# Splitting FFN weights by two GpSimd DMAs and one ScalarE pass

## The chip, the core and the metric

The kernel runs on one core of a Trainium2 chip. The metric is the time of one execution on the device, in microseconds, taken as the median of several runs. A core has engines that run side by side and meet through semaphores: TensorE (PE in the profile, PEld for its weight loads), VectorE (DVE), ScalarE (ACT), GpSimd (POOL) and SyncE (SP), and 16 DMA engines that move data between HBM and SBUF. Each engine works through its own instructions in a fixed order; an instruction whose inputs are late holds up all that stand behind it on that engine.

## The reference: what is computed

Two trunk layers over 512 tokens of width 1024, in float32. The first mixes tokens by attention (four global and four windowed heads, 256 context tokens beside them), the second by a Fourier transform over tokens and channels. Each layer ends with a gated ConvFFN of width 2816, and every sub-layer lies between RMS norms with shift, scale and gate from a conditioning vector. The change lies in the ConvFFN:

```
def conv_ffn(h, w_up, conv_w, conv_b, w_down):
    u = h @ w_up                                  # 512 x 1024 times 1024 x 5632
    up = jnp.pad(u, ((0, 0), (1, 1), (0, 0)))
    u = up[:, :-2] * conv_w[0] + up[:, 1:-1] * conv_w[1] + up[:, 2:] * conv_w[2] + conv_b
    gate, val = jnp.split(u, 2, axis=-1)
    return (jax.nn.silu(gate) * val) @ w_down     # 512 x 2816 times 2816 x 1024
```

## The kernel before

**Products in two parts.** TensorE multiplies numbers of the rounded type float32r. To keep float32 accuracy each operand is split into a high part h (the value rounded to float32r) and a low part l (what the rounding left, rounded again), and a product is the sum of three matmuls, h h, h l and l h, into one PSUM bank. `mm3` (lines 97 to 99) issues them: L97 and L98 read the high part of the weights, L99 the low part. For the weights the high part is called `wh`, the low part `wl`.

**The split.** `split` (line 119) makes both parts from a float32 tile: ScalarE copies the tile into h with the rounding cast, and VectorE (or, where a call says so, GpSimd) subtracts h from the tile into l. Both are recorded on line 120. `held` ties an instruction behind the last fence that was set on its engine, so that the planner doesn't draw it ahead of a norm between two sub-layers.

**Weights and their buffers.** A weight tile goes from HBM into a buffer `raw` (line 127, three buffers of up to 8 KB per partition, loads issued by SP), is split into a pair `wh`, `wl` (line 132, five pairs of 4 KB each), and is multiplied. The three `raw` buffers are shared by everything that is loaded to be split: up weights, down weights, the weights of the attention and the Fourier layer, the sums that a seven-product step makes of its weights, and the tiles of the modulation matrix that VectorE multiplies in a GEMV (lines 388 and 391). Buffers of one name are given out in program order, each as soon as one comes free.

**The FFN.** `ffn` (line 1057 on) runs over 22 chunks fi of 128 inner channels. For each chunk there is a gate and a value tile of `w_up`, 1024 x 128 each (512 KB), loaded as one tile of 1 MB. A chunk is computed in one of two ways. A *plain* step takes the two tiles with 24 matmuls of 512 columns each. A *seven-product* step (`seven_products`) takes both tiles together as a 2 x 2 block product with seven block products instead of eight: VectorE makes sums of weight blocks in a second `raw` buffer, four pairs are split from them, and there are 84 matmuls of 256 columns, with copies of PSUM halves by ScalarE (lines 1020 to 1030) between them. The list `SEVEN` names the chunks of the second kind: 5, 6, 8, 10, 12, 14, 15, 17, 18, 20 in layer 0, and 8, 9, 11, 12, 14, 15, 17, 18, 20 in layer 1. Chunks 0 to 2 are done at the start of the FFN in another way, interleaved with the norm before it, so 9 plain steps are left in layer 0 and 10 in layer 1. After a step, ScalarE and VectorE make the convolution from PSUM (lines 1079 to 1082) and the gating (1092, 1093), and the result is split into the tiles that the down product reads.

The chunks stand in three groups, `GROUPS`: 8, 6 and 8 chunks. When a group is done, its share of the down product follows: eight tiles d of `w_down`, each of as many 128 x 128 blocks as the group has chunks (512 KB for 8 chunks, 24 matmuls; 384 KB for 6, 18 matmuls), added up in `yT`. `weights(d)` loads and splits such a tile. The last group (`end`) is done in two halves of the tokens and uses other buffers for some of its tiles.

**The order of the work.** The program is written as one stream; a planner gives each engine its order beforehand, by program order as priority and by modelled times of when inputs and buffers are ready. In layer 0 the GEMV of the second layer's modulation is woven into the plain steps and the down tiles (`pump(gem, ...)`).

Of the kernel before, what the change touches and what calls it, by code (L numbers as in the profile page):

```python
# [14 lines left out]
AF = mybir.ActivationFunctionType  # L15
ALU = mybir.AluOpType
# [3 lines left out]
P = 128  # L20
D = 1024
KC = D // P
T = 512
# [51 lines left out]
def kernel(ctx: ExitStack, tc: tile.TileContext, a):  # L75
    nc = tc.nc
    V, S, G, PE, SY = nc.vector, nc.scalar, nc.gpsimd, nc.tensor, nc.sync
# [15 lines left out]
    def f(ap):  # L93
        return ap.bitcast(F32)
# [19 lines left out]
    def held(i):  # L114
        if i.ins.engine in fences:
            tc.add_manual_dep(i.ins, fences[i.ins.engine], mybir.DependencyInfo(
                mybir.DependencyClass.NoSync, mybir.DependencyReason.DATA), reason="fence")

    def split(h, l, src, eng=V):
        i = S.copy(out=h, in_=src), eng.tensor_tensor(out=l, in0=src, in1=f(h), op=ALU.subtract)  # L120
        for j in i:
            held(j)

    cp = ctx.enter_context(tc.tile_pool(name="cp", bufs=1))
    wp = ctx.enter_context(tc.tile_pool(name="wp", bufs=1))

    def raw(shape, src):
        t = mk(wp, shape, F32, "raw", 3)
        SY.dma_start(out=t, in_=src)
        return t  # L130

    def wpair(shape):
        return mk(wp, shape, F32R, "wh", 5), mk(wp, shape, F32R, "wl", 5)
# [300 lines left out]
    def pump(it, n=1):  # L434
        for _ in range(n):
            next(it, None)
# [12 lines left out]
    with ExitStack() as es:  # L449
# [29 lines left out]
        with ExitStack() as e1:  # L479
# [187 lines left out]
            for ps, (sh, sl, t, b) in zip(acc, tiles):  # L667
                S.copy(out=Vv[:, b, 0:256], in_=ps[:, 256:512])
                src = ps[:, 0:256].unsqueeze(1)
# [53 lines left out]
            for g, kind in enumerate(["kb", "vb", "qa"]):  # L723
# [5 lines left out]
                for sh, sl, t0, kb in (blocks if kind[0] != "q" else blocks[:2]):  # L729
                    ps = mk(pps, [P, 2, 256], F32, "mm", 6)  # L730
# [23 lines left out]
        with ExitStack() as e2:  # L754
# [79 lines left out]
            for head in range(8):  # L834
# [6 lines left out]
                for j in range(TT):  # L841
                    qs = slice(j * P, (j + 1) * P)
                    ps = S0.pop() if S0 else mk(aps, [P, 1024], F32, "S", 2)
# [107 lines left out]
    def up_weights(l, pairs, fis, eng=V):  # L951
        for fi in fis:
            r = raw([P, 2, KC, P], a["w_up"][l, fi])
            for i in range(2):
                wh, wl = pairs([P, KC, P])
                split(wh, wl, r[:, i, :, :], eng)
                yield [(wh[:, k, :], wl[:, k, :]) for k in range(KC)]
# [99 lines left out]
    def ffn(l, xp, ready, pre, mid, gem, plain=None):  # L1057
# [4 lines left out]
        def up_mm(ps, w, sl):  # L1062
            for k, ((wh, wl), (bh, bl)) in enumerate(zip(w, H)):
                mm3(ps[:, sl], wh, wl, bh[:, sl], bl[:, sl], k == 0, k == KC - 1)
# [109 lines left out]
        for gi, (f0, nch) in enumerate(GROUPS):  # L1174
            end = gi == len(GROUPS) - 1
            for fi in range(max(f0, FIRST), f0 + nch):
                if fi == SUMS[l]:
                    bs = seven_inputs(xp)
                if fi in SEVEN[l]:
                    cc = [conv(fi, i, u, None, i == 1) for i, u in enumerate(seven_products(l, fi, pps, bs))]  # L1180
                else:
                    cc = []
                    for i, w in enumerate(up_weights(l, wpair, [fi])):
                        ps = mk(pps, [P, T], F32, "mm", 6)
                        up_mm(ps, w, slice(0, T))
                        cc.append(conv(fi, i, ps))
                gated(fi, cc[0], cc[1], f0)
                if l == 0 and fi not in SEVEN[l]:
                    pump(gem, GP[0])
            g_ = [gs[fi] for fi in range(f0, f0 + nch)]  # L1190
            ws = {}

            def part(d, hs, ps=None):
                ps, sl = y_mm(pps, ws[d], g_, hs, True, ps)
                if gi == 0:
                    S.copy(out=yT[:, d, sl], in_=ps[:, sl])
                else:
                    V.tensor_tensor(out=yT[:, d, sl], in0=yT[:, d, sl], in1=ps[:, sl], op=ALU.add)
                if end:
                    ys.add(pps, yT[:, d, sl], hs)  # L1200

            def weights(d):
                r = raw([P, nch, P], a["w_down%d" % gi][l, d])
                wh, wl = (xp.spare if end and 4 <= d < 7 else wpair)([P, nch, P])
                split(wh, wl, r)
                ws[d] = [(wh[:, c, :], wl[:, c, :]) for c in range(nch)]


            hs = {d: [0, 1] if not end or d == 0 else [0] for d in range(KC)}
            begun = {}  # L1210
            if end:
                pump(gem, 100)
                fence()
            keep = dict(fences)
            fences.clear()
            for d in range(2):
                weights(d)
            fences.update(keep)
            for d in range(2):
                begun[d] = y_mm(pps, ws[d], g_, hs[d], False)[0]  # L1220
            for d in range(KC):
                if d not in ws:
                    weights(d)
                part(d, hs[d], begun.get(d))
                if gem is not None and not end:
                    pump(gem, GP[1])
            if end:
                mid(ys)
                for d in range(1, KC):
                    part(d, [1])  # L1230
# [12 lines left out]
    with ExitStack() as es:  # L1243
# [147 lines left out]
        for d in range(KC):  # L1391
            wh, wl = w_f.pop() if w_f else fourier_weights(d)
# [138 lines left out]
```

## Time and profile before

| | us |
|---|---|
| median of three runs | 1158.47 |
| lowest and highest of them | 1157.93 and 1159.31 |
| profiled execution | 1163.01 |
| its span, first to last instruction | 1161.2 |

The profile shows one execution, with the busy time of each engine, the span in slices, the DMA queues, the chain of work that ended last, and groups of instructions by line, engine and tile. A row such as `wh<-raw` is the instruction that writes tile `wh` from tile `raw`; buffer numbers are left out, so all five pairs appear under one name. In a timeline each row is start, duration, engine, line, operation, tiles and shape, and in brackets the time that the engine stood idle before it and the instruction that released it. A busy TensorE isn't TensorE at its peak: matmuls overlap, so the rate is read from the distance of two starts.

### The profile page before, as it was taken

How to read it: one execution, taken by the hardware profiler on the slowest of the kernel's cores; microseconds unless marked ns; L12 is line 12 of the kernel's file. 1: busy time of each engine (PE TensorE's matmuls, PEld its weight loads, DVE VectorE, ACT ScalarE, POOL GpSimd, SP SyncE). 2: the span in 40 equal slices, each digit the busy share in tenths (PEclk: the TensorE clock that was granted, in tenths of full speed). 3: DMA queues.
4: the chain of work that ended last, by engine and by line, in shares of the span. 5: the costliest groups of instructions: out<-in, count | busy, mean ns of one | idle time of the engine just before them, and what ended most of it. 6: DMA issues, size and time to landing. Idle time of an engine off the chain costs nothing.

```text
span 1161.2 us, 19052 instructions
## 1 busy us (share of the span) xinstructions
PE 1119.1 (96%) x7658; PEld 965.9 (83%) x7658; DVE 860.7 (74%) x1402; ACT 577.2 (50%) x1025; POOL 169.1 (15%) x181
## 2 busy tenths in 40 slices
PE   7999999999999999999899998989999999999995
PEld 4689889669888978887798898869888888899895
DVE  5573776675679966987899658878997497579745
ACT  4342355566665634551465445556843365265442
POOL 1122433212420000000000143430000000000023
PEclk9899999999999999999999999999999999999998
DMA  9532110775202455445524400531217233223212
GB/s 371 201 123 73 37 37 1 290 267 205 74 27 85 146 183 222 175 163 179 189 86 156 145 1 19 185 124 38 73 53 274 73 109 110 76 106 109 91 56 73
DMA packets 29440, 145.31 MB, mean 125 GB/s; under 512 B 2980, under 2 KB 7716, under 8 KB 16424
## 3 DMA queue, kind: packets, MB, share of 16 engines
q1 hardware_dynamic: 29352, 144.09, 35.1%
q8 instruction: 60, 0.98, 0.3%
q14 instruction: 28, 0.23, 0.1%
HBM read 141.98 MB, written 2.10 MB: 124 GB/s over the span
## 4 chain that ended last, share of the span: by engine, by line
PE 80%; DVE 9%; ACT 4%; DMA 3%; issue 1%; POOL 1%; DVEq 0%; SPq 0%; POOLq 0%; ACTq 0%
PE mm L97 22%; PE mm L99 21%; PE mm L98 21%; PE PT L798 2%; PE gm L417 1%; DMA raw<-in_w_up 1%; DVE md_t L288 1%; ACT wh L120 1%; PE O L97 1%; DVE wl L120 1%; PE S L97 1%; PE gm L97 1%; PE O L98 1%; PE gm L98 1%; PE gm L99 1%
## 5 line engine op out<-in xcount | busy, mean ns | idle before, releaser
L120 ACT CAST wh<-raw 128x1024 fp32r<-128x1024 f32 (+2 forms) x189 | 179.9, 965 | 160.1 <-PE mm L98 70.5
L120 DVE TENSOR_TENSOR wl<-raw,wh 128x1024 fp32r<-128x1024 f32 (+3 forms) x177 | 200.4, 1140 | 73.3 <-ACT wh L120 73.1
L97 PE MATMUL mm<-hh,wh 128*128 128x256 f32 (+2 forms) x652 | 220.9, 339 | 2.4 <-ACT wh L120 1.9
L99 PE MATMUL mm<-hh,wl 128*128 128x256 f32 (+2 forms) x652 | 219.0, 336 | 0.2 <-DVE wl L120 0.2
L98 PE MATMUL mm<-hl,wh 128*128 128x256 f32 (+2 forms) x652 | 218.7, 335 | 0.0
L97 PEld LDWEIGHTS mm<-hh,wh 128*128 128x128 f32 x652 | 122.9, 188 | 19.3 <-ACT wh L120 2.3
L99 PEld LDWEIGHTS mm<-hh,wl 128*128 128x128 f32 x652 | 123.1, 189 | 14.9 <-issue 0.4
L263 POOL TENSOR_TENSOR gacc<-gacc,sq 128x256 f32<-128x256 f32 (+1 forms) x35 | 30.2, 864 | 718.4 <-ACT sq L261 717.5
L98 PEld LDWEIGHTS mm<-hl,wh 128*128 128x128 f32 x652 | 123.1, 189 | 13.7
L97 PE MATMUL mm<-xh,wh 128*128 128x512 f32 (+1 forms) x368 | 131.5, 358 | 0.2 <-ACT wh L120 0.2
L98 PE MATMUL mm<-xl,wh 128*128 128x512 f32 (+1 forms) x368 | 130.7, 355 | 0.1
L99 PE MATMUL mm<-xh,wl 128*128 128x512 f32 (+1 forms) x368 | 129.9, 354 | 0.0
L97 PE MATMUL mm<-zh,wh 128*128 128x256 f32 x304 | 87.1, 287 | 1.2 <-ACT wh L120 1.2
L99 PE MATMUL mm<-zh,wl 128*128 128x256 f32 x304 | 84.9, 279 | 0.4 <-DVE wl L120 0.4
L98 PE MATMUL mm<-zl,wh 128*128 128x256 f32 x304 | 84.9, 279 | 0.0
L97 PEld LDWEIGHTS mm<-xh,wh 128*128 128x128 f32 x368 | 69.1, 188 | 13.1 <-issue 1.6
L98 PEld LDWEIGHTS mm<-xl,wh 128*128 128x128 f32 x368 | 69.1, 188 | 11.2 <-DVE xl L120 0.3
L99 PEld LDWEIGHTS mm<-xh,wl 128*128 128x128 f32 x368 | 69.0, 188 | 10.9
L1079 ACT ACTIVATE cv<-mm,cols 128x512 f32<-128x512 f32 x64 | 49.7, 777 | 27.8 <-PE mm L99 21.6
L97 PEld LDWEIGHTS mm<-zh,wh 128*128 128x128 f32 x304 | 57.6, 189 | 5.1 <-ACT sq L1025 2.9
L99 PEld LDWEIGHTS mm<-zh,wl 128*128 128x128 f32 x304 | 57.6, 190 | 0.7 <-DVE wl L120 0.6
L391 DVE SCALAR_TENSOR_TENSOR gacc<-raw,scol,gacc 128x1024 f32<-128x1024 f32 x42 | 53.8, 1282 | 5.8 <-DMA raw<-in_mod_r 5.3
(386 smaller groups left out, 2655.0 us busy)
## 6 DMA issues: line engine op xcount, KB each, us to landing
raw<-in_w_up SPq DMA_DIRECT2D x44, 1024.0 KB, 4.9
raw<-in_mod_r SPq DMA_DIRECT2D x24, 1024.0 KB, 5.0
raw<-in_mod_p SPq DMA_DIRECT2D x16, 1024.0 KB, 4.9
raw<-in_w_down SPq DMA_DIRECT2D x32, 512.0 KB, 3.8
raw<-in_w_in SPq DMA_DIRECT2D x6, 1024.0 KB, 4.8
raw<-in_w_down SPq DMA_DIRECT2D x16, 384.0 KB, 3.1
raw<-in_w_out SPq DMA_DIRECT2D x4, 1024.0 KB, 4.9
raw<-in_w_f SPq DMA_DIRECT2D x8, 512.0 KB, 3.5
```

Source lines behind the costliest of these rows:

```text
L97: i = PE.matmul(out, lhsT=ah, rhs=bh, start=start, stop=False, skip_group_check=skip)
L98: PE.matmul(out, lhsT=ah, rhs=bl, start=False, stop=False, skip_group_check=skip)
L99: return i, PE.matmul(out, lhsT=al, rhs=bh, start=False, stop=stop, skip_group_check=skip)
L120: i = S.copy(out=h, in_=src), eng.tensor_tensor(out=l, in0=src, in1=f(h), op=ALU.subtract)
L263: G.tensor_tensor(out=self.acc[:, sl], in0=self.acc[:, sl], in1=sq[:, sl], op=ALU.add)
L288: m = V.scalar_tensor_tensor(out=t, in0=yT[:, k, hs], scalar=der[:, l, gi, k:k + 1], in1=R, op0=ALU.mult, op1=ALU.mult)
L391: held(V.scalar_tensor_tensor(out=acc, in0=w[:, i, :], scalar=scol[:, 0, k:k + 1], in1=acc, op0=ALU.mult, op1=ALU.add))
L417: PE.matmul(ps[32 * q:32 * q + 32, :], lhsT=spad[:, k, :], rhs=w[:, q * T:(q + 1) * T], start=k == 0, stop=k == KC - 1)
L798: PE.transpose(out=pt[:, j * P:(j + 1) * P], in_=Ps[j][:, off:off + P], identity=ident)
L1079: S.activation(out=cv, in_=ps, func=AF.Identity, bias=bc, scale=wc[1])
```

## The change

A new function, `split_in`, makes the pair straight from HBM, without a `raw` buffer and without VectorE: a DMA of GpSimd casts the tile into h, ScalarE writes -h into l, and a second DMA of GpSimd reads the tile from HBM again and adds it to l. The plain steps use it for both of their tiles, and the down tiles of the first two groups for theirs: 38 and 32 tiles in the two layers together. Chunks 0 to 2, the seven-product steps and the last down group keep the old way. The scratch space for GpSimd's DMA descriptors grows from 1024 to 2048 bytes of each partition.

```diff
+    def split_in(h, l, src):
+        G.dma_start(out=h, in_=src)
+        held(S.activation(out=l, in_=f(h), func=AF.Copy, scale=-1.0))
+        G.dma_start(out=l, in_=src, accum_op=ALU.add)
...
                 else:
                     cc = []
-                    for i, w in enumerate(up_weights(l, wpair, [fi])):
+                    for i in range(2):
+                        wh, wl = wpair([P, KC, P])
+                        split_in(wh, wl, a["w_up"][l, fi, :, i])
                         ps = mk(pps, [P, T], F32, "mm", 6)
-                        up_mm(ps, w, slice(0, T))
+                        up_mm(ps, [(wh[:, k, :], wl[:, k, :]) for k in range(KC)], slice(0, T))
                         cc.append(conv(fi, i, ps))
...
             def weights(d):
-                r = raw([P, nch, P], a["w_down%d" % gi][l, d])
                 wh, wl = (xp.spare if end and 4 <= d < 7 else wpair)([P, nch, P])
-                split(wh, wl, r)
+                src = a["w_down%d" % gi][l, d]
+                if end:
+                    split(wh, wl, raw([P, nch, P], src))
+                else:
+                    split_in(wh, wl, src)
                 ws[d] = [(wh[:, c, :], wl[:, c, :]) for c in range(nch)]
...
-    nc = bacc.Bacc("TRN2", target_bir_lowering=False, num_devices=1, dynamic_dma_scratch_size=1024)
+    nc = bacc.Bacc("TRN2", target_bir_lowering=False, num_devices=1, dynamic_dma_scratch_size=2048)
```

## Prediction

> **What bounds the kernel now.** I read the head of the page first, then its chain, then the table of windows, then the timeline of the places where TensorE stood still.
>
> ```profile
> span 1161.2 us, 19052 instructions
> PE 1119.1 (96%) x7658; PEld 965.9 (83%) x7658; DVE 860.7 (74%) x1402; ACT 577.2 (50%) x1025; POOL 169.1 (15%) x181
> PE 80%; DVE 9%; ACT 4%; DMA 3%; issue 1%; POOL 1%; DVEq 0%; SPq 0%; POOLq 0%; ACTq 0%
> ```
>
> TensorE works for 96% of the span and makes 80% of the chain that ended last. The whole program offers 42 us in which it stands idle, so work taken from VectorE is worth something only where TensorE waits for it. The profiled execution took 1163.0 us (span 1161.2, 1.8 around it), 4.5 above the median of the three timed runs, 1158.5. I work out the difference in the profile and put it on the median.
>
> The change touches the two FFNs behind their first steps: 358 to 650 us (layer 0) and 817 to 1101 us (layer 1). Windows there (PE, PEld, DVE, ACT, POOL busy, then clock, DMA share, GB/s):
>
> ```profile
> 540.00:560.00 20.00, 18.35 (x85) 13.80 (x83) 13.75 (x16) 3.15 (x5) 0.00 (x0) 1.00 0.76 263
> 560.00:580.00 20.00, 18.16 (x135) 17.55 (x136) 18.29 (x22) 12.76 (x20) 0.00 (x0) 0.91 0.44 163
> 940.00:960.00 20.00, 20.00 (x123) 17.62 (x123) 17.82 (x25) 11.23 (x18) 0.00 (x0) 1.00 0.15 53
> 1020.00:1040.00 20.00, 19.93 (x152) 18.76 (x151) 14.42 (x19) 11.52 (x19) 0.00 (x0) 1.00 0.30 106
> ```
>
> In layer 1 TensorE has no holes; VectorE may be at 89%, nobody waits for it. The one place with time to win is 558 to 566 us in layer 0, where step 14 (seven products) follows the down tiles of the second group. The timeline of TensorE (start, duration, in brackets the idle time before and who ended it), and for comparison the starts of steps 14, 15 and 16 in layer 1:
>
> ```profile
> 558.12 0.40 PE L99 MATMUL mm<-xh,wl 128*128 128x512 f32 x1
> 560.39 0.39 PE L97 MATMUL mm<-hh,wh 128*128 128x256 f32 x1 [1.87 <-ACT wh L120]
> 562.13 0.38 PE L97 MATMUL mm<-zh,wh 128*128 128x256 f32 x1 [1.24 <-ACT wh L120]
> ...
> 565.99 0.41 PE L98 MATMUL mm<-zl,wh 128*128 128x256 f32 x1
> 566.21 0.40 PE L99 MATMUL mm<-zh,wl 128*128 128x256 f32 x1
> 566.67 0.28 PE L99 MATMUL mm<-zh,wl 128*128 128x256 f32 x1
> 566.79 0.28 PE L97 MATMUL mm<-zh,wh 128*128 128x256 f32 x1
> ...
> 573.79 0.28 PE L97 MATMUL mm<-hh,wh 128*128 128x256 f32 x1
> ```
>
> ```profile
> 1016.00 0.28 PE L97 MATMUL mm<-hh,wh 128*128 128x256 f32 x1
> 1026.38 0.28 PE L97 MATMUL mm<-hh,wh 128*128 128x256 f32 x1
> 1036.78 0.40 PE L97 MATMUL mm<-hh,wh 128*128 128x512 f32 x1
> 1037.24 0.40 PE L99 MATMUL mm<-hh,wl 128*128 128x512 f32 x1
> ```
>
> From the end of the last down tile's stream (558.12 and about 0.23 for 512 columns) to step 15 (573.79) layer 0 needs 15.44 us; the same step in layer 1 needs 10.38 (1016.00 to 1026.38). The loss is 5.06 us, and it has two parts: two waits for the weights, 3.1 us, and behind them matmuls that follow each other at 0.22 us in place of 0.12 until 566.4. The clock column says 0.91 for that window: a stop of 3 us is followed by some 3.6 us at half speed, 1.6 us more. Who was late there, from the chain in order of time:
>
> ```profile
> 551.31 1.21 DVE gacc L391
> 552.53 7.17 DMA raw<-in_w_up
> 559.72 1.22 DVE raw L986
> ```
>
> The load of step 14 went out only at 552.53, when the modulation GEMV (L391) gave a `raw` buffer back; three buffers serve the GEMV, the down tiles and the up weights.
>
> **The change, part by part.** *Removed:* the loads of 19 plain steps and 32 down tiles from SP and from `raw`, and 70 subtractions from VectorE.
>
> ```profile
> L120 ACT CAST wh<-raw 128x1024 fp32r<-128x1024 f32 (+2 forms) x189 | 179.9, 965 | 160.1 <-PE mm L98 70.5
> L120 DVE TENSOR_TENSOR wl<-raw,wh 128x1024 fp32r<-128x1024 f32 (+3 forms) x177 | 200.4, 1140 | 73.3 <-ACT wh L120 73.1
> ```
>
> At 1.14 us each that is 80 us of VectorE. By the windows this buys nothing in layer 1. In layer 0 `raw` is left to the GEMV and to the seven-product steps, so the load of step 14 can go out when a GEMV tile of three loads ago is read, not after eight down tiles in between; the eight down tiles, 33.6 us at the rate below, are its cover. I book the 5.06 us in full. Next in line there are the weight pairs: a matmul of 512 columns takes 0.23 us (1036.78 to 1037.24 is two), so a down tile of this group (18 matmuls) 4.2 us and a tile of 24 matmuls 5.6; the pairs of the step's first two weight tiles come free four and three down tiles, 16.8 and 12.6 us, before it begins. That is enough for a cast and a subtraction.
>
> The larger descriptor scratch (1024 to 2048 bytes of each partition) is no instruction and is booked at nothing. *Kept:* ScalarE's pass. It writes -wh into wl in place of casting raw into wh; same shape, so the same 0.97 us and the same count.
>
> *Added:* per tile a casting DMA and an adding DMA of GpSimd. The queue table shows that before had no queue of that kind, so their price has to be bounded from the loads of SP:
>
> ```profile
> q1 hardware_dynamic: 29352, 144.09, 35.1%
> q8 instruction: 60, 0.98, 0.3%
> q14 instruction: 28, 0.23, 0.1%
> raw<-in_w_up SPq DMA_DIRECT2D x44, 1024.0 KB, 4.9
> raw<-in_w_down SPq DMA_DIRECT2D x32, 512.0 KB, 3.8
> raw<-in_w_down SPq DMA_DIRECT2D x16, 384.0 KB, 3.1
> DMA to landing us min/median/max: 4.7/4.9/8.1
> DMA to landing us min/median/max: 2.8/3.6/6.1
> ```
>
> (The last two are w_up and w_down, from issue to landing.) *Throughput* is no problem: in a down group a tile is read every 4.2 to 5.6 us, two transfers take some 3 us of the engines. GpSimd computes nothing in these stretches:
>
> ```profile
> 1111.24 0.74 POOL L263 TENSOR_TENSOR gacc<-gacc,sq 128x256 f32<-128x256 f32 x1 [343.70 <-ACT sq L261]
> ```
>
> *Latency* is what decides. Five pairs wh/wl exist, taken in program order as they come free. In an unbroken run of plain or down tiles a pair comes free four tiles ahead of its use, 17 to 22 us. But a seven-product step uses four pairs in 10.4 us. When it begins, four are spoken for by its own weights, and the fifth, which goes to the first tile of the plain step behind it, comes free just then, with the last product or tile of the step before. Layer 1 shows it: step 14 ends at 1026.38, and the cast that waited for that is
>
> ```profile
> 1026.47 1.05 ACT L120 CAST wh<-raw 128x1024 fp32r<-128x1024 f32 x1 [0.35 <-PE mm L98]
> ```
>
> which I read as step 16's first tile (the ninth pair from step 14 on; step 15 has seven products). TensorE wants its wl with the third matmul of step 16, at 1037.24: 10.86 us after the pair came free. Before, this chain is a cast of 1.05 and a subtraction of 1.14, with the load done long ahead. After, it holds everything:
>
> release to issue 0.1; casting DMA 3.8 (the 512 KB row); more for GpSimd's issue than for SP's, between 0 and 0.74 (the short instruction above), say 0.4; landing to ScalarE 0.1; waiting behind another pass of ScalarE 0.3 (busy 11.5 of 20 us in that window, in pieces of up to 1.05); pass 1.05; to GpSimd 0.1; issue 0.4; adding DMA 3.8 to 4.9. For the last I take 4.9, the row of 1 MB, because the transfer reads 512 KB of weights and the 512 KB of wl that it adds to. Sum 11.15. The ends lie far apart: 2.8 for each transfer and no extra issue make 7.0, and 6.1, 8.1 and two issues of 0.74 make 17.3. I stay by the medians, since most loads land there, but they are not the whole of it: a late landing costs in full while an early one gives nothing back, and SP's loads of 1 MB run beside these; I add 0.5. That is 11.65 against 10.86, **0.8 us late**.
>
> The Trainium skill, "Collectives: The Full Stack", section "The bandwidth ceiling: the fold count and why AG ≠ RS ≠ AR", says that an add in the DMA datapath costs no cycles of its own but needs two source reads, which halves its rate. No run so far shows it; by it the last term stays at 4.9, and without it it would be 3.8. The skill's "DMA: Bandwidth & Descriptors", section "Measured (HBM→SBUF, 128 partitions, SWDGE, issued from GpSimd)", gives 6.15 us for 1 MB where SP's row has 4.9; with that estimate in the last place the lateness would be 2.0 us and the total 1178.
>
> Plain steps behind a seven-product step are 7, 9, 11, 13, 16, 19, 21 in layer 0 and 10, 13, 16, 19, 21 in layer 1: twelve. 12 x 0.8 = 9.6 us. Each second tile (pair free one product, 1.5 us, later, needed 5.6 us later) has over 3 us in hand and is booked at nothing.
>
> *Added waits.* GpSimd's adding DMA waits for ScalarE; behind it stand only casting DMAs of later tiles. ScalarE's pass waits for the casting DMA; behind it stand the copies of the seven products (L1020 to L1030) and the convolution passes (L1079), and TensorE waits for the copies' PSUM halves. I price that inside the 0.5.
>
> Sum: 9.6 - 5.06 = +4.5 us; the profile would read some 1167.5, the median **1163.0**.
>
> **Rivals.** *The chain fits.* If the adding DMA costs no more than a copy (3.8), the chain is 10.55 with everything else as above, under 10.86, and the gain stands alone: 1153.4. For it: uncontended loads of 384 KB land in 2.8; DVE and SP are relieved. Against: two issues of another engine, never seen here. It decides at 10.86 us from release to landing.
>
> *Both cancel.* Lateness of 0.23 to 0.61 us each leaves the total within 0.2% of 1158.5, which is about what a measurement of this kernel can tell from no change.
>
> *The adding DMA is slow.* If it needs as long as the longest w_up load, 8.1, tiles come 4 us late, and behind stops over 3 us the clock drops as at 563: 12 x (4.0 + 1.6) - 5 gives 1221. Nothing in the trace speaks for it except that nothing excludes it; 0.06, within slower.
>
> *The gain does not come.* If step 14's load stays behind the GEMV's loads, because these too are served in program order from `raw`, the total is 1168. I hold 0.15 of that, within slower mostly.
>
> **How the numbers follow.** The forecast (tiles late by more than 0.6 us) has 0.46 and is the likeliest; the chain that fits has 0.37; the middle 0.17. The range starts at 1153, the gain alone, and ends at 1178, tiles late by 2 us, which is both DMAs 0.6 us over what I took, still far inside the 6.1 and 8.1 of the rows; some 0.13 lies above, 0.05 below. The forecast's own range is 1161 to 1178.
>
> **What would show it.** In the profile after: a GpSimd queue with 140 transfers; 70 subtractions fewer; in layer 0 at the start of step 14 no stop and no slow matmuls (right) or the same 5 us (the gain failed); at the starts of the twelve plain steps a gap of 0.5 to 1.5 us before the third matmul, L99, ended by the adding DMA (right), or none (the chain fits). From release to landing the first tile should take 11 to 12.5 us, the adding DMA about 1 us more than the casting one. It would be wrong if gaps stand at L97 (then the casting DMA or the queue order is late), or in the middle of down groups.

## The result, and the profile after

The kernel after takes 1251.64 us (median of 4 runs, 1247.48 to 1258.07) against 1158.2 before (4 runs, 1156.82 to 1159.31): a ratio of 1.0812, 95% interval 1.0763 to 1.0861. It is slower by 93 us, where the prediction had +4.5 and a range up to 1178. The profiled execution of after has a span of 1248.5 us, 87.3 more than before. Lines of the code behind `split_in` move by six: the copies of the seven products are now L1026 to L1036, the GEMV L394 to L411; in `split_in` the casting DMA is L126, ScalarE's pass L127, the adding DMA L128. From the page of after, its head, the DMA queues (packets, MB, share of the 16 engines' time) and the chain:

```profile
span 1248.5 us, 19201 instructions
...
PE 1146.7 (92%) x7658; PEld 987.7 (79%) x7658; DVE 789.3 (63%) x1332; ACT 577.9 (46%) x1025; POOL 271.5 (22%) x321
...
q0 software_dynamic: 20160, 69.21, 24.7%
q1 hardware_dynamic: 22008, 109.49, 24.4%
...
PE 21%; issue 18%; DMA 5%; DVE 3%; POOL 3%; ACT 1%; DVEq 0%; POOLq 0%; ACTq 0%; SPq 0%
```

The shares of this chain add up to half of the span only, so I go by the waits.

VectorE has the 70 subtractions fewer that were foretold (1402 to 1332 instructions, 71 us), and it helps nobody. GpSimd's queue moves 69 MB in as much engine time as SP's takes for 109. What TensorE waits for in the products of the FFN, from the waits of after (us in total, times, longest):

```profile
PE mm L97 <- ACT sq L1031: 39.7, 12, 5.4
PE mm L97 <- ACT xh L120: 9.7, 3, 6.4
PE mm L99 <- DMA wl<-in_w_down: 6.4, 3, 3.4
...
PE mm L99 <- DMA wl<-in_w_up: 2.1, 1, 2.1
```

The foretold wait, L99 for the adding DMA at a plain step, is the last row, once. In its place stands one that the prediction had priced inside half a microsecond: the first row, in just the foretold number of places, twelve. One of them, from the timeline of after (step 9 of layer 1, seven products, begins at 984.33; step 10 is plain):

```profile
986.14 0.33 SPq L135 DMA_DIRECT2D raw<-in_w_up  x1
...
984.75 0.55 POOL L126 DMA_DIRECT2D wh<-in_w_up  x1 [25.93 <-PE mm L99]
986.24 0.54 POOL L126 DMA_DIRECT2D wh<-in_w_up  x1 [0.93 <-DVE wl L120]
990.47 0.89 POOL L128 DMA_DIRECT2D wl<-in_w_up  x1 [3.69 <-ACT wl L127]
...
995.15 1.06 ACT L127 ACTIVATE wl<-wh 128x1024 fp32r<-128x1024 f32 x1 [4.55 <-DMA wh<-in_w_up]
996.11 0.35 ACT L1031 COPY sq<-mm 128x256 f32<-128x256 f32 x1
...
991.16 0.28 PE L99 MATMUL mm<-hh,wl 128*128 128x256 f32 x1
996.52 0.58 PE L97 MATMUL mm<-zh,wh 128*128 128x256 f32 x1 [5.08 <-ACT sq L1031]
...
1002.02 0.41 PE L98 MATMUL mm<-zl,wh 128*128 128x256 f32 x1
1002.23 0.34 PE L99 MATMUL mm<-zh,wl 128*128 128x256 f32 x1
```

The casts of step 10's two tiles go out at 984.75 and 986.24, SP's load of 1 MB for the next seven-product step at 986.14. The trace's row for the second cast alone, from issue to landing:

```profile
DMA to landing us min/median/max: 8.9/8.9/8.9
```

ScalarE waits for it in the pass (995.15), and the copy L1031 stands behind the pass in ScalarE's order. TensorE needs the PSUM half that this copy empties: it stands from 991.4 to 996.5, and after that its matmuls follow each other at 0.21 us until the end of the step.

The second and third rows of the waits lie in the down groups. From the timeline of after, second group of layer 1:

```profile
1045.64 0.90 POOL L126 DMA_DIRECT2D wh<-in_w_down  x1
1055.55 0.86 POOL L128 DMA_DIRECT2D wl<-in_w_down  x1 [9.01 <-ACT wl L127]
1056.09 0.88 POOL L126 DMA_DIRECT2D wh<-in_w_down  x1
...
1054.19 0.85 ACT L127 ACTIVATE wl<-wh 128x768 fp32r<-128x768 f32 x1 [5.45 <-DMA wh<-in_w_down]
...
1061.34 0.84 ACT L127 ACTIVATE wl<-wh 128x768 fp32r<-128x768 f32 x1 [5.64 <-DMA wh<-in_w_down]
1062.09 0.60 ACT L120 CAST xh<-cv 128x512 fp32r<-128x512 f32 x1
...
1062.74 0.80 PE L97 MATMUL mm<-xh,wh 128*128 128x512 f32 x1 [6.40 <-ACT xh L120]
```

Two queues in fixed order take turns in waiting. GpSimd's addition (1055.55) waits for ScalarE's pass (1054.19), which waits for a casting DMA (1045.64). Behind the addition on GpSimd stands the next casting DMA (1056.09); ScalarE's next pass (1061.34) waits for that, and behind the pass stands the cast of the last activations, without which TensorE can't go on.

Two sums account for 83.9 of the 87.3 us. The four down groups of the first two chunk groups (first matmul of the group to first matmul of the next step), in us:

| down group | before | after | e5 | e3 |
|---|---|---|---|---|
| layer 0, first | 46.7 | 48.4 | 46.7 | 46.7 |
| layer 0, second | 37.9 | 44.5 | 42.0 | 35.6 |
| layer 1, first | 44.8 | 51.1 | 46.5 | 45.8 |
| layer 1, second | 33.6 | 42.4 | 35.0 | 35.2 |
| sum | 163.0 | 186.4 | 170.1 | 163.2 |

They lose 23.4 us. The steps around them, from the first plain step of each layer to its last down group and by the same starts, take 413.2 before and 473.7 after: 60.5 us, 5.0 for each of the twelve places. Of these, 3.3 are the stop (39.7 in 12). Most of the rest are slow matmuls: behind nine of the twelve stops the granted clock reads 0.5 for 3.4 or 6.8 us.

### The profile page after: what moved, and what is told of

Its sections match the earlier page's. It is cut to its first block, busy times and chain, and to the rows that moved or that the text cites. A ratio compares the mean times of both kernels' runs of the same rounds, so it can differ in the third digit from the quotient of the medians.

```text
span 1248.5 us, 19201 instructions
## 1 busy us (share of the span) xinstructions
PE 1146.7 (92%) x7658; PEld 987.7 (79%) x7658; DVE 789.3 (63%) x1332; ACT 577.9 (46%) x1025; POOL 271.5 (22%) x321
## 3 DMA queue, kind: packets, MB, share of 16 engines
q0 software_dynamic: 20160, 69.21, 24.7%
## 4 chain that ended last, share of the span: by engine, by line
PE 21%; issue 18%; DMA 5%; DVE 3%; POOL 3%; ACT 1%; DVEq 0%; POOLq 0%; ACTq 0%; SPq 0%
PE mm L97 7%; PE mm L98 6%; PE mm L99 6%; DMA wh<-in_w_up 4%; POOL wh L126 1%; POOL wl L128 1%; DVE md_t L294 1%; DMA raw<-in_w_up 1%; DMA wh<-in_w_down 1%; DVE hl L352 1%; DVE xT L296 0%; DVE wl L120 0%; POOL gacc L269 0%; PE mm L183 0%; PE misc L217 0%
## 5 line engine op out<-in xcount | busy, mean ns | idle before, releaser
L97 PE MATMUL mm<-hh,wh 128*128 128x256 f32 (+2 forms) x652 | 222.7, 342 | 0.4 <-ACT sq L1028 0.4
L99 PE MATMUL mm<-hh,wl 128*128 128x256 f32 (+2 forms) x652 | 220.7, 338 | 2.1 <-DMA wl<-in_w_up 2.1
L120 DVE TENSOR_TENSOR wl<-raw,wh 128x1024 fp32r<-128x1024 f32 (+1 forms) x107 | 120.5, 1134 | 86.5 <-ACT wh L120 86.1
L120 ACT CAST wh<-raw 128x1024 fp32r<-128x1024 f32 (+1 forms) x119 | 110.2, 944 | 106.1 <-PE mm L98 61.7
L127 ACT ACTIVATE wl<-wh 128x1024 fp32r<-128x1024 f32 (+1 forms) x70 | 70.0, 1007 | 169.6 <-DMA wh<-in_w_down 106.0
L97 PE MATMUL mm<-xh,wh 128*128 128x512 f32 (+1 forms) x368 | 134.5, 366 | 9.7 <-ACT xh L120 9.7
L99 PE MATMUL mm<-xh,wl 128*128 128x512 f32 (+1 forms) x368 | 132.7, 361 | 6.4 <-DMA wl<-in_w_down 6.4
L97 PEld LDWEIGHTS mm<-hh,wh 128*128 128x128 f32 x652 | 124.8, 191 | 17.1 <-ACT sq L1028 2.8
L99 PEld LDWEIGHTS mm<-hh,wl 128*128 128x128 f32 x652 | 125.2, 192 | 16.5 <-DMA wl<-in_w_up 2.6
L97 PE MATMUL mm<-zh,wh 128*128 128x256 f32 x304 | 93.4, 307 | 41.9 <-ACT sq L1031 39.7
L97 PEld LDWEIGHTS mm<-zh,wh 128*128 128x128 f32 x304 | 63.4, 209 | 45.8 <-ACT sq L1031 42.7
L99 PE MATMUL mm<-zh,wl 128*128 128x256 f32 x304 | 90.8, 299 | 2.1 <-DVE wl L120 2.1
L98 PE MATMUL mm<-zl,wh 128*128 128x256 f32 x304 | 90.9, 299 | 0.0
L97 PEld LDWEIGHTS mm<-xh,wh 128*128 128x128 f32 x368 | 70.5, 192 | 24.3 <-ACT xh L120 11.0
L99 PEld LDWEIGHTS mm<-xh,wl 128*128 128x128 f32 x368 | 70.3, 191 | 18.6 <-DMA wl<-in_w_down 7.7
L126 POOL DMA_DIRECT2D wh<-in_w_up x38 | 22.4, 592 | 281.3 <-PE mm L99 241.9
L1086 DVE SCALAR_TENSOR_TENSOR cv<-mm,cols,cv 128x511 f32<-128x511 f32 x64 | 47.7, 746 | 46.2 <-ACT cv L1085 46.2
L128 POOL DMA_DIRECT2D wl<-in_w_up x38 | 33.8, 890 | 157.3 <-ACT wl L127 128.3
```

What stands on the lines that cost most here:

```text
L97: i = PE.matmul(out, lhsT=ah, rhs=bh, start=start, stop=False, skip_group_check=skip)
L98: PE.matmul(out, lhsT=ah, rhs=bl, start=False, stop=False, skip_group_check=skip)
L99: return i, PE.matmul(out, lhsT=al, rhs=bh, start=False, stop=stop, skip_group_check=skip)
L126: G.dma_start(out=h, in_=src)
L127: held(S.activation(out=l, in_=f(h), func=AF.Copy, scale=-1.0))
L128: G.dma_start(out=l, in_=src, accum_op=ALU.add)
```

## The experiments

The theories, in short. 1a: ScalarE's order is all of it. 1b: the chain of a tile (cast, pass, addition) is longer than the time between a pair's release and its use behind a seven-product step, and ScalarE's order only decides where TensorE stands. 2: the tiles are late whoever makes the pass. 3: the addition is dear. 4: the alternation on GpSimd makes the down groups slow. 5: the transfers crowd each other wherever they stand. 6 and 7: GpSimd's queue is slow by itself, or isn't. Where there was one execution, I hold differences under 10 us of time for nothing: the runs of the kernel before lay between 1154.1 and 1164.8.

**e1: the pass on GpSimd.**

```diff
-        held(S.activation(out=l, in_=f(h), func=AF.Copy, scale=-1.0))
+        held(G.tensor_scalar(out=l, in0=f(h), scalar1=-1.0, scalar2=None, op0=ALU.mult))
```

> The pass that writes -h is moved from ScalarE to GpSimd; the two DMAs and their tiles are the same. Theory 1 (ScalarE's fixed order): the time is lost because the pass stands in ScalarE's order ahead of the PSUM copies of the seven products and of the cast of xh, and waits there for a casting DMA that lands some 6 us after its issue. In the profile of after TensorE waits 39.7 us for the copy sq at L1031 and 9.7 us for xh; with the slow matmuls behind the stops I put it at some 65 us. Without the wait in ScalarE both waits go under 3 us, and the time falls to 1175 to 1205; what is left are second halves of tiles that come late (L99 waiting for an adding DMA). Theory 2 (the tiles themselves are late): the two DMAs and the pass need longer than the plain step gives them, and whoever makes the pass, TensorE stands as long, only at L99 and L97 of the plain steps and the down tiles: 1235 to 1265.

1315.67 us, ratio 1.1334 (1.1282 to 1.1385): slower still, and outside both ranges. From its waits:

```profile
PE mm L99 <- DMA wl<-in_w_up: 60.1, 15, 7.6
PE mm L99 <- DMA wl<-in_w_down: 45.3, 13, 5.3
```

Both waits for ScalarE are gone, as theory 1 said, and the time isn't: now the additions are late at L99. Part of that is the edit's own, since a pass takes 2.84 us on GpSimd (198.4 us in 70) against 1.01 on ScalarE in after (70.0 us in 70), and GpSimd issues nothing meanwhile.

**e2: one half of the change each.** In e2_down_only the plain steps go back to `up_weights`; in e2_plain_only the down tiles go back to `split` and `raw`.

> Only the down tiles of the first two groups are split by the two DMAs; the plain steps are split the old way, from raw. Theory 1: the stops in the seven-product steps (some 42 us in after, before the slow matmuls) are all gone; the down groups keep theirs (some 18 us with step 14 of layer 0, and slow matmuls): 1180 to 1195. Theory 2: the plain steps carry little of the loss by themselves and transfers that crowd each other carry it: 1200 to 1230.

> Only the plain steps are split by the two DMAs; the down tiles are loaded to raw and split the old way. Theory 1: the stops behind the copy at L1031 stay, ten to twelve of 2 to 5 us, with slow matmuls behind them: 1210 to 1235. Theory 2: with the down tiles off the GpSimd queue the transfers come sooner: 1175 to 1205.

1200.39 and 1227.61 (one execution each, before 1159.98): 40 us for the down tiles, 68 for the plain steps. In e2_plain_only the first row of its waits is

```profile
PE mm L97 <- ACT sq L1031: 45.7, 12, 6.3
```

so the plain steps do this alone, without the down tiles' transfers, as theory 1 expected. The down tiles lose more alone than theory 1 gave them and stand at the lower end of theory 2; together the halves lose 108, more than the whole, so part of each loss hides behind the other.

**e3: no addition.** The second DMA copies in place of adding, so l holds the whole tile and not the rest.

```diff
-        G.dma_start(out=l, in_=src, accum_op=ALU.add)
+        G.dma_start(out=l, in_=src)
```

> The second DMA writes the tile to l without adding (so l holds the tile in place of the rest, and the low part of the result is something else). Theory 1: the second DMA lands 5.5 to 6.3 us after its issue as before, and it isn't what ScalarE waits for; time within 1% of after, 1239 to 1264. Theory 3 (the addition is dear: it reads what it adds to, and takes the bandwidth of the engines twice): landings of the second DMA fall by 1 us or more, the software queue's share of the engines falls from 24.7% to under 20%, and casting DMAs land earlier too: under 1225.

1226.26: 25 us less than after, just above the bound that was set for theory 3, and far from no change. Its queue table, the landings of both DMAs of a plain step, and its first wait:

```profile
q0 software_dynamic: 20160, 69.21, 18.3%
```

```profile
wh<-in_w_up POOLq DMA_DIRECT2D x38, 512.0 KB, 5.3
wl<-in_w_up POOLq DMA_DIRECT2D x38, 512.0 KB, 4.8
```

```profile
PE mm L97 <- ACT sq L1031: 41.1, 12, 6.7
```

18.3% of 1224.4 us are 224 us of all 16 engines for 140 transfers, 1.60 each. In after it is 24.7% of 1248.5, 308 us; if the casts take as long in both runs, the 84 more belong to 70 additions, which thus take 2.81 us each, 1.75 times a cast. Without the additions all that the down groups had lost is back (table above, last column), and the plain steps' waits are as they were. So there are two losses with two causes: what the additions take from the DMA engines in the down groups, something else in the plain steps.

**e4: the passes behind the copies.** `copies` holds the copies L1031 and L1036 of the last seven-product step.

```diff
+        if n is not None:
+            follow(i, copies[n])
...
+                        split_in(wh, wl, a["w_up"][l, fi, :, i], i if fi - 1 in SEVEN[l] else None)
```

> Where a plain step follows a seven-product step, ScalarE's pass for the plain step's first tile is put behind that step's copy at L1031, and the one for the second tile behind the last copy; all else as in after. Theory 1a (the order on ScalarE is all of it): the 39.7 us of waits for that copy and the slow matmuls behind them go and little comes in their place: 1180 to 1205. Theory 1b (the chain of a tile is itself longer than the step gives it, and ScalarE's order only decides where TensorE stands): the waits for the copy fall under 5 us, and L99 of the plain steps waits for the adding DMA instead, 2 to 4 us at each of twelve places; some of the loss comes back, not most: 1215 to 1245.

1232.56. Its waits, without the rows that before has too:

```profile
PE mm L99 <- DMA wl<-in_w_up: 39.0, 13, 4.5
...
PE mm L97 <- ACT sq L1031: 2.4, 1, 2.4
```

The 39.7 us at the copy have become 39.0 at L99 of the plain step, 3.0 us in each place: theory 1b. That the two sums are so near is partly chance. Some of the 39.0 is the edit's own, as the pass now waits for the copy even where the cast has landed: for the first tile in nine of the twelve places, by 1.1 to 2.7 us, 15.5 in all. The lateness without that can be read from after itself: from the start of a seven-product step to the third matmul behind it there are 10.38 us and two matmuls of 0.23, and the first tile's addition lands 0.3 to 5.0 us after that in the twelve places, 32.4 in all. So by after itself some four fifths of the 39.7 are the chain's and the rest is the order's; by e4 less its own part, 23.5 us, it would be three fifths. Either way the chain has the greater part. Most of the 19 us that the time came down are not the plain steps': the planner also set GpSimd's order anew, and the down groups fell from 186.4 to 172.0.

**e5 and e6: the next cast ahead of the addition, in down groups; and both edits.**

```diff
+        if down and adds:
+            follow(adds[-1], i)
```

(`i` is the casting DMA of the tile, `adds[-1]` the addition of the tile before.)

> In the down groups the casting DMA of the next tile is put ahead of the adding DMA of a tile in GpSimd's order; nothing else is moved. In after an adding DMA that waits for ScalarE holds back the next casting DMA, for which ScalarE then waits: at 1055.55 an addition goes out after 9.0 us of waiting, and the casting DMA behind it at 1056.09, though its pair had been free since 1049.2. Theory 4 (this alternation makes the down groups slow): the four down groups, 44 to 51 us each in after, come down by 3 to 6 us each: 1228 to 1240. Theory 5 (the transfers crowd each other, the order on the queue matters little): 1243 to 1258, the groups as long as in after.

> Both edits together. Theories 1a and 4: under 1190. Theories 1b and 4: 1200 to 1230, with stops at L99 of the plain steps. Theories 1b and 5: 1215 to 1250.

e5 took 1235.86, and the down groups come down by 16.3 us (table), each by 1.7 to 7.4: theory 4, of the size expected in all. e6 took 1232.13, a little above what was expected of the two: its down groups sum to 169.8 and its waits at L99 are 42.3 us, so both edits had cured the same groups, and neither the plain steps.

**e7 and e13: six pairs and two `raw` buffers, in after and in before.**

```diff
-        return mk(wp, shape, F32R, "wh", 5), mk(wp, shape, F32R, "wl", 5)
+        return mk(wp, shape, F32R, "wh", 6), mk(wp, shape, F32R, "wl", 6)
```

> Six pairs in place of five, and two raw buffers in place of three, which is the same space; the changed splitting as in after. The first tile behind a seven-product step then has its pair a tile earlier, and the second has it when the first had it. Theory 1b (the chain is too long for the time between a pair's release and its use): both chains fit, the waits for the copy at L1031 fall from 39.7 us to under 15, and the time to 1190 to 1220, unless the two raw buffers make the loads of the seven-product steps late (waits for casts of L120). Theory 5 (crowded transfers): the same transfers in the same steps, 1235 to 1260.

> Control for the run with six pairs: the kernel before with six pairs and two raw buffers. With the old split every tile needs a raw buffer, so the loads come late: 1175 to 1230. Theory 1b: the new split with six pairs (1254.3) then costs under 50 us over this control, against 93 with five pairs. Theory 5: it costs 80 us or more over it.

1254.32 and 1237.02. By itself e7 was a miss: no faster, though the copy's wait fell to 15.4 us. The control tells why. Two `raw` buffers cost the old kernel 77 us; above it the new split costs 17 us in place of 93. That fits theory 1b but doesn't price it: in the control every tile needs one of the two `raw` buffers, in e7 the tiles of the new split need none, and in a kernel that stands still so often elsewhere some lateness is hidden.

**e8 and e9: seven-product steps first in each group, in after and in before.**

```diff
-SEVEN = [(5, 6, 8, 10, 12, 14, 15, 17, 18, 20), (8, 9, 11, 12, 14, 15, 17, 18, 20)]
+SEVEN = [(5, 6, 8, 9, 10, 14, 15, 16, 17, 18), (8, 9, 10, 11, 14, 15, 16, 17, 18)]
```

> The splitting is that of after; only the list of chunks is put in another order: in each group the seven-product steps come first and the plain steps behind them (layer 0: 5, 6, 8, 9, 10, 14 to 18; layer 1: 8 to 11, 14 to 18), so that the number of both and of all transfers stays, but 5 plain steps follow a seven-product step in place of 12. Theory 1b (a pair comes free too late for the chain, and only behind a seven-product step): the waits for the copy at L1031 fall from 39.7 us in 12 places to some 17 in 5, and with the slow matmuls behind them the time falls by 25 to 40 us, to 1210 to 1228, if the same list costs the kernel before nothing. Theory 5 (the transfers crowd each other wherever they stand): the waits move to the plain steps behind plain steps, 1240 to 1260.

> Control for the last run: the kernel before with the same list. Four and five seven-product steps in a row need more of VectorE than before; if it keeps up, 1155 to 1170; if not, stops at L97 for casts of L120, 1170 to 1190.

1240.47 and 1170.89. By its time alone e8 falls to theory 5, but the list costs the old kernel 11 us. Over its control the split costs 69.6 us, 24 less than 93, just short of the 25 to 40 expected. The copy's wait falls to 8.5 us:

```profile
PE mm L97 <- ACT sq L1031: 8.5, 5, 7.3
```

These are not the five places that were counted; only two of them are, with 7.8 us. But with the plain step's own waits for its DMAs (L97 and L99) each of the five places behind a seven-product step has its stop, of 7.3, 5.4, 2.7, 2.2 and 1.5 us by the timeline, 19.2 in all where 17 were expected; plain steps behind plain ones have 0.8 at most. The down groups, which now stand behind two or three plain steps in a row, took some back: they sum to 195.2 us against 162.6 in the control, and their wait for `xh` grew from 9.7 to 18.9 us.

**e10: the old loads through GpSimd's queue.**

```diff
-        SY.dma_start(out=t, in_=src)
+        q.dma_start(out=t, in_=src)
```

> The kernel before, with the raw loads of the plain steps (1 MB) and of the down tiles of the first two groups issued by GpSimd in place of SP, without cast or add; the split is the old one. Theory 6 (GpSimd's queue is slow by itself): from issue to landing these take as long as the casting DMAs of after, over 5 us for 512 KB, over 6 for 1 MB. Theory 7 (the crowd makes them late, the queue doesn't): within 0.6 us of SP's 3.6 and 4.9. By both the time stays near the kernel before, 1155 to 1175, as the loads have slack.

1164.43, with the larger descriptor scratch too, so that this isn't what costs. From its DMA table:

```profile
raw<-in_w_up SPq DMA_DIRECT2D x25, 1024.0 KB, 4.9
...
raw<-in_w_up POOLq DMA_DIRECT2D x19, 1024.0 KB, 5.1
raw<-in_w_down POOLq DMA_DIRECT2D x16, 512.0 KB, 3.7
```

GpSimd's queue is as quick as SP's (theory 7). The Trainium skill, "DMA: Bandwidth & Descriptors", section "Measured (HBM→SBUF, 128 partitions, SWDGE, issued from GpSimd)", has 6.15 us for 1 MB; this kernel's 5.1 is what holds here.

**e11, e15, e16, e17: step 14 in the kernel before.** e11 moves its load ahead by three loads; the others take GEMV parts out of its way, and e17, the simplest, leaves out two `pump` calls (their parts are done with the rest of the GEMV, ahead of the last down group):

```diff
-                if gem is not None and not end:
+                if gem is not None and not end and not (gi == 1 and d > 5):
```

> The kernel before, with one line moved: the load of step 14 of layer 0 takes its raw buffer ahead of the seventh down tile's multiplication, three loads earlier than before. If the late load alone makes the stop of 5.1 us there, the time falls by 2 to 5 us, to a ratio of 0.996 to 0.998; if the buffer for the sums or the GEMV's tiles are then the late ones, within 0.2% of before or slower.

> The kernel before; the GEMV makes no progress at the last three down tiles of the second group of layer 0 and two parts in place of one at the plain steps 16, 19 and 21. If the GEMV's loads and VectorE passes ahead of step 14 make its 5.1 us, the stop at 558 to 566 us goes and nothing comes in its place: ratio 0.995 to 0.998. If the later GEMV parts stand in the way elsewhere: 0.999 to 1.003.

> The kernel before; the GEMV makes no progress at the last three down tiles of the second group of layer 0, and three parts more at step 21, behind which the third group's down tiles follow. If the 5.1 us at step 14 are the GEMV's doing and nothing waits for it behind step 21: ratio 0.995 to 0.997. If the later parts hold up the down tiles' loads (they share the raw buffers): 0.999 to 1.003.

> The kernel before; only the last two down tiles of that group go without the GEMV, and the two parts left over are done where the rest of the GEMV is, ahead of the third group's down tiles. Two loads fewer ahead of step 14 free its buffers some 8 us earlier: if that is enough, ratio 0.995 to 0.998, if the sums still wait for VectorE, 0.998 to 1.001.

Ratios to before: e11 1.0025 (1.0012 to 1.0038), stops of 1.7 and 0.8 us in the down tiles ahead of step 14 and 2.5 behind it; e15 0.9997 (0.9980 to 1.0014), stops of 1.6 and 2.4 us at step 20, behind one of the moved parts; e16 0.9970 (0.9954 to 0.9987); e17 0.9958 (0.9940 to 0.9976). From the timeline of e17, the end of the second group and step 14:

```profile
557.96 0.40 PE L99 MATMUL mm<-xh,wl 128*128 128x512 f32 x1
558.19 0.28 PE L97 MATMUL mm<-hh,wh 128*128 128x256 f32 x1
558.31 0.28 PE L98 MATMUL mm<-hl,wh 128*128 128x256 f32 x1
```

No stop: 1154.96 us, 4.9 less than before. e16 and e17 beat both kernels, and they have nothing of the change.

**e12: the new split only where a pair is free four tiles ahead.** Steps 3 and 4 of layer 0 and 3 to 7 of layer 1.

```diff
+                    own = fi - 1 not in SEVEN[l]
+                    ws2 = [] if own else up_weights(l, wpair, [fi])
...
```

> The new split is used only in plain steps that don't follow a seven-product step (3 and 4 in layer 0, 3 to 7 in layer 1: 14 of the 38 tiles); the other plain steps and all down tiles are split the old way. Theory 1b (late only where a pair comes free one step before its use): no stops at these steps, 1154 to 1168, within 0.6% of before. Theory 5 (the transfers are late wherever they stand): 14 of 38 of the 67 us that the plain steps cost alone, some 25 us: 1175 to 1190.

1168.67, ratio 1.0066 (1.0041 to 1.0091), just outside of what theory 1b allows (1168, 0.6%) and far from theory 5. Its landings:

```profile
wh<-in_w_up POOLq DMA_DIRECT2D x14, 512.0 KB, 6.7
wl<-in_w_up POOLq DMA_DIRECT2D x14, 512.0 KB, 6.8
```

The transfers are as slow here as anywhere, and no matmul waits for one: with four tiles of lead nobody notices. What costs the 0.66% (7.7 us) lies elsewhere: the first down group of layer 1 takes 52.1 us in place of 44.8, with a stop of 4.3, and there is a stop of 2.2 at step 5 of layer 0, neither with a transfer of the new split as its releaser. In that group the cast of the last activations is late, and ahead of it VectorE's order has a part of the GEMV that waited for its own load:

```profile
881.04 1.28 DVE L397 SCALAR_TENSOR_TENSOR gacc<-raw,scol,gacc 128x1024 f32<-128x1024 f32 x1 [1.27 <-DMA raw<-in_mod_r]
...
889.91 0.62 ACT L120 CAST xh<-cv 128x512 fp32r<-128x512 f32 x1 [2.79 <-DVE cv L1099]
```

So it looks like another order that the planner gave VectorE, which no run tested.

**e14: the first tile's addition ahead of the second tile's cast,** behind a seven-product step; otherwise as e4, with the first pass free from the second copy on.

```diff
+        if n == 1:
+            follow(j, adds[-1])
```

> As the run with the pass put behind the copies, but behind a seven-product step GpSimd issues the first tile's adding DMA ahead of the second tile's casting DMA, and the first tile's pass may run from the second copy on. Crowding theory: the first tile's addition, alone on the engines but for SP's load, lands in 5.4 to 5.9 us in place of 7, its chain takes some 11.5 us from the cast's issue in place of 14, and the waits at L99 of the plain steps fall from 39 us to under 22; the second tile is later by its later cast: 1212 to 1228. Lone-chain theory (each transfer is that slow by itself): the first tile as late as before and the second later: 1232 to 1255.

1254.95: the time is where the lone-chain theory had it, but for another reason. From its waits:

```profile
PE mm L99 <- DMA wl<-in_w_up: 45.1, 21, 4.7
```

The five chains of layer 1 show both halves. The first tile, from the cast's issue to the addition's landing, now takes 10.9 to 12.0 us in place of 12.9 to 14.7 in e4, and TensorE waits for it 0.3 to 1.6 us, 0.8 on average. Part of the difference is the hold that e4 had put on the pass. The rest is the crowd: in after, without that hold, the same five take 12.7, 13.5, 12.9, 12.4 and 10.95 us, here 12.0, 11.3, 10.9, 11.6 and 10.97, and only the last had no load of SP's beside it. So in these five the second tile's transfers delay the first only where such a load runs too. (In layer 0, beside the GEMV's loads, TensorE still waits up to 3.3 us for a first tile.) But the second tile, cast 6 us later, is now late by 2.3 to 4.7. There is barely time for one chain behind a seven-product step, and none for two.

## Why the prediction was wrong

**The step that failed** is the sum for the first tile, 11.65 us against 10.86, with the sentence ahead of it that throughput is no problem. It is a sum of transfers each alone. Where little runs beside them it holds: at step 20 of layer 1, where no load of SP's comes beside them, the trace has

```profile
1165.50 0.55 POOL L126 DMA_DIRECT2D wh<-in_w_up  x1 [14.23 <-PE mm L99]
...
1170.89 0.90 POOL L128 DMA_DIRECT2D wl<-in_w_up  x1 [3.37 <-ACT wl L127]
```

with 3.9 and 5.6 us to landing (booked: 3.8 and 4.9), 10.95 in all and 11.3 from the release of the pair. But the change puts three or four transfers at one place: two casts 1.5 us apart, two additions that cost 1.75 casts each, and the 1 MB of the next seven-product step. The medians became 6.3 and 6.1 us. e14, which takes the second tile's transfers away from the first tile's, brings TensorE's waits for the first tile in layer 1 down to the 0.8 us that was predicted. The lateness of the first tile (worked out under e4) sorts itself by what ran beside it. In three places no load of SP's was under way but the tail of one: 0.5, 0.3 and 0.4 us late (seven-product steps that begin at 525.92, 672.93 and 1165.19), less than the 0.8 of the prediction; the stops of 1.7 to 1.9 us there are ScalarE's order. In the other nine a load of SP's for a seven-product step, the GEMV or a down tile ran in the midst of the chain: 2.0 to 5.0 us late. The mean is 2.7 in place of 0.8; ScalarE's order adds 0.6, which makes the stop of 3.3, and the other 1.7 are mostly the slow matmuls, which the prediction had kept for a rival. Twelve times 5.0 is 60, not 9.6.

The Trainium skill's rule that an add needs two source reads ("Collectives: The Full Stack", section "The bandwidth ceiling: the fold count and why AG ≠ RS ≠ AR") fits e3: 1.75 times the engine time, not quite twice. I had used it for one addition's latency and not for what it takes from its neighbours.

**The rest, point by point.** The place was right: twelve plain steps behind seven-product steps, bound to the release of the pairs (e8, e12). Both signs of being wrong that the prediction had named came: stops at L97, and stops in the down groups. *Added waits*, priced inside the 0.5, were wrong twice. From the waits of ScalarE in after:

```profile
ACT wl L127 <- DMA wh<-in_w_down: 106.0, 22, 16.0
...
ACT wl L127 <- DMA wh<-in_w_up: 57.1, 28, 5.4
```

ScalarE stood 163 us for casts; for the plain steps that mostly moved the lateness ahead of the step (e4). On GpSimd, where I saw "only casting DMAs of later tiles" behind the addition, just these were what ScalarE needed next: 16 us in the down groups (e5). *Down groups* were booked at nothing and lost 23.4; e3 shows that without the additions even the bad order costs nothing there. *The second tile*, wanted 5.6 us behind the first, has no 3 us in hand: in after it lands 1.2 to 2.3 us too late in seven of the twelve places, for a step that had kept its time. *The low end of the chain*, 7.0, adds up to 7.25 by its own terms; nothing hangs on it. *The gain at step 14* was booked at 5.06 us, and by the same measure 1.3 came. From the timeline of after, the second group of layer 0:

```profile
573.32 0.91 POOL L126 DMA_DIRECT2D wh<-in_w_down  x1
...
585.38 0.84 ACT L127 ACTIVATE wl<-wh 128x768 fp32r<-128x768 f32 x1 [12.99 <-DMA wh<-in_w_down]
586.13 0.35 ACT L405 COPY gacc<-misc 128x256 f32<-128x256 f32 x1
...
588.88 0.39 PE L99 MATMUL mm<-xh,wl 128*128 128x512 f32 x1
589.11 0.38 PE L409 MATMUL misc<-con,gacc 128*128 128x128 f32 x2
...
589.91 0.16 DVE L411 TENSOR_TENSOR mods<-misc,cols 128x8 f32<-128x8 f32 x1
589.99 0.74 DVE L394 TENSOR_SCALAR gacc<-raw,scol 128x1024 f32<-128x1024 f32 x1
...
593.29 1.22 DVE L992 TENSOR_TENSOR raw<-raw 128x1024 f32<-128x1024 f32 x1
```

The load of step 14 goes out at 575.57 and lands 9.5 us later, ten ahead of the step, as the prediction had it. But the sums of the step (L992) stand behind the GEMV on VectorE. The GEMV's next part (L394) stands there behind L411, which reads TensorE's transposes (L409), and these stand in TensorE's order behind the matmuls of a down tile, until 589.11. The copy L405, held behind a pass that waits 13 us for a cast, is done before that. From the end of the last down tile's stream to step 15 it takes 14.1 us (595.25 to 609.37) where before took 15.44 and layer 1 took 10.38. So the late load was one cause of the 5 us and VectorE's GEMV another, which the prediction had left out: moving the load alone gained nothing (e11), and fewer GEMV parts ahead of the step did (e17).

What stays open: the part of SP's loads in the slow landings is read from nine places against three, and no run took these loads away; and the order that costs e12 its 0.66% was read from one trace.

## What to carry to other kernels

A transfer's latency, read where it ran alone, is a lower bound: before adding up a chain, list what else the change sends at the same moment, and count an adding DMA nearly twice. A new wait on an engine with a fixed order is priced by what stands behind it there and on the next queue, not by the wait itself; but when such a wait moves to another place and most of it stays, as from after to e4, the order is the lesser cause, and the time between a buffer's release and its use the greater. Take off first what the edit itself holds back. And relief for an engine that nobody waits for is worth nothing, however large.

## What the runs showed of the hardware

- An adding DMA from HBM into SBUF occupied the DMA engines 1.75 times as long as a casting one of the same size (2.81 and 1.60 us on average over tiles of 512 and 384 KB, from the difference of after and e3); with no load of SP's beside them, 512 KB landed in 5.6 us against 3.9 (step 20 of layer 1).
- A plain load through GpSimd's queue lands about as soon as through SP's (1 MB: 5.1 and 4.9 us, e10), though its issue takes 0.53 us of GpSimd; the issue of an addition takes 0.89 (after).
- Short stops of TensorE can be followed by slow matmuls: behind nine of the twelve stops at the copy in after (1.7 to 5.4 us) the granted clock read 0.5 for 3.4 or 6.8 us, behind three (1.8, 2.3 and 2.8 us) it stayed at 1.0, so the length alone doesn't tell. At 996.52 TensorE went on at 0.21 us for 128x256 in place of 0.12 until the step ended, 6 us later.
